# Half a row of x in the last step as two transfers of 88 and 40 partitions, and the first result stored in three pieces

## The chip, the cores and the metric

The kernel runs on one core of a Trainium2 chip. The metric is the device time of one execution in microseconds. All data is float32. The engines that matter are VectorE (DVE in the profile), ScalarE (ACT), SyncE (SP), which issues most transfers, and the core's sixteen DMA engines, which carry every transfer between HBM and SBUF.

## The reference

x and y have the shape 8 × 4096 × 512. Only the diagonal of x·yᵀ is needed: 8 × 4096 dot products of 512 elements, then a softmax over the 4096 of each batch.

```
gram = np.matmul(x, y.transpose(0, 2, 1))
diag = np.diagonal(gram, axis1=1, axis2=2)
diag = diag - diag.max(axis=-1, keepdims=True)
exp = np.exp(diag)
return (exp / exp.sum(axis=-1, keepdims=True)).astype(np.float32)
```

## The kernel before

The eight batches are worked in two sets of four. A set fills the 128 partitions: each batch has 32 partitions (G), and each partition holds 128 consecutive rows (C) of its batch. A set is read in four steps of 32 rows (R), so there are eight steps (S), t = 0 to 7. A step loads 32 rows of x into one of two buffers (`xs`) and 32 rows of y into the only y buffer (`ys`), 8.4 MB each: 64 KB for each partition.

Steps 0 to 5 load x and y whole. VectorE multiplies (`products`, L75) and sums the rows (`sums`, L78), and ScalarE sums the last two rows (`sums_act`, L83). ScalarE copies the last six rows of y aside (L125), so that `ys` comes free sooner. Step 6 loads y in two parts.

Step 7, the last, is loaded in ever smaller parts, x and y in turn, all issued on SyncE's queue: x rows 0–14, y rows 0–16, x 15–22, y 17–24, x 23–27, y 25–28, x 28–29, y 29–30. Then come x row 30 with the first 192 elements of row 31 (L162, 352 KB), y row 31, and the last 320 elements of x row 31 (L164, 160 KB). Each row is one instruction on VectorE, which multiplies and sums (`dot`, L87), as soon as both its rows are there. Row 31 is two instructions, of 192 and of 320 elements; the second takes up the first one's result through an extra element, where y has a 1. Ahead of row 29 the largest of the earlier dot products is taken (`largest`, L100).

The first set's softmax is done early, in steps 3 and 4. Its result, `res[0]`, is stored by SyncE after all loads are issued, in five pieces of 32, 32, 32, 16 and 16 partitions (L173). After the last dot product come the second set's softmax (`exps`, `normalize`) and its store from ScalarE's queue (L175).

The semaphores that tell of a transfer's completion are eight, used in turn by SyncE's and ScalarE's transfers alike. A transfer is not issued before the one that had its semaphore, the eighth before it, has landed. Queued transfers start in the order of their issue.

Of the kernel before, what the change touches and what calls it, by code (L numbers as in the profile page):

```python
# [1 line left out]

# [5 lines left out]


@with_exitstack
def kernel(
    ctx: ExitStack,
    tc: tile.TileContext,
    x: bass.AP,
    y: bass.AP,
    out: bass.AP,
):
    nc = tc.nc
    ctx.enter_context(tc.manual_schedule())  # L20
    f32 = mybir.dt.float32
    Alu = mybir.AluOpType
    Act = mybir.ActivationFunctionType
    X = mybir.AxisListType.X
    B, N, D = x.shape
    P = nc.NUM_PARTITIONS
    G = 32
    Q = P // G
    C = N // G
    R = 32  # L30
    K = 6
    W = 2
    F = 17
    V = 8
    L = 320
    S = B // Q * (C // R)


    xv = x.rearrange("(s b) (j c) d -> s (b j) c d", b=Q, j=G)
    yv = y.rearrange("(s b) (j c) d -> s (b j) c d", b=Q, j=G)  # L40
    ov = out.rearrange("(s b) (j c) -> s (b j) c", b=Q, j=G)

    big = ctx.enter_context(tc.tile_pool(name="big", bufs=1))
    small = ctx.enter_context(tc.tile_pool(name="small", bufs=1))


    xs = [big.tile([P, R * D + i], f32, name=f"xs{i}") for i in range(2)]
    ys = big.tile([P, R * D + 1], f32, name="ys")
    side = big.tile([P, K * D], f32, name="side")

    diag = [small.tile([P, C + i], f32, name=f"diag{i}") for i in range(B // Q)]
    res = [small.tile([P, C], f32, name=f"res{i}") for i in range(B // Q)]

    def columns(t, r0, n):
        c0 = t % (C // R) * R + r0
        return slice(c0, c0 + n)

    def rows(tile_, r0, n):
        return tile_[:, r0 * D : (r0 + n) * D].rearrange("p (r d) -> p r d", d=D)

    def dots_of(t, r0, n):
        return diag[t * R // C][:, columns(t, r0, n)]

    def load(tile_, view, t, r0, n):
        nc.sync.dma_start(out=rows(tile_, r0, n), in_=view[t * R // C, :, columns(t, r0, n), :])  # L65

    def load_x(t, r0, n):
        load(xs[t % 2], xv, t, r0, n)

    def load_y(t, r0, n):  # L70
        load(ys, yv, t, r0, n)

    def products(t, r0, n, yt):
        xt = rows(xs[t % 2], r0, n)
        nc.vector.tensor_tensor(out=xt, in0=xt, in1=yt, op=Alu.mult)  # L75

    def sums(t, r0, n):
        nc.vector.tensor_reduce(out=dots_of(t, r0, n), in_=rows(xs[t % 2], r0, n), axis=X, op=Alu.add)  # L78

    def sums_act(t, r0, n):  # L80
        for r in range(r0, r0 + n):
            row = xs[t % 2][:, r * D : (r + 1) * D]
            nc.scalar.activation(out=row, in_=row, func=Act.Copy, accum_out=dots_of(t, r, 1))  # L83

    def dot(t, e0, n, got):
        xt = xs[t % 2][:, e0 : e0 + n]
        nc.vector.scalar_tensor_tensor(  # L87
            out=xt, in0=xt, scalar=1.0, in1=ys[:, e0 : e0 + n], op0=Alu.mult, op1=Alu.mult, accum_out=got
        )

    def over_quadrant(name, column, op, negate=False):

        got = small.tile([P, 1], f32, name=name)
        nc.vector.tensor_reduce(  # L94
            out=got, in_=column.to_broadcast([P, G]), axis=X, op=op, negate=negate, apply_transpose=True
        )
        return got

    def largest(out, d):
        nc.vector.tensor_reduce(out=out, in_=d, axis=X, op=Alu.max)  # L100

    def exps(i, d):
        mxp = small.tile([P, 1], f32, name=f"mxp{i}")
        largest(mxp, d)
        nmx = over_quadrant(f"nmx{i}", mxp, Alu.max, negate=True)
        sump = small.tile([P, 1], f32, name=f"sump{i}")
        nc.scalar.activation(out=res[i], in_=diag[i][:, :C], func=Act.Exp, bias=nmx, scale=1.0, accum_out=sump)  # L107
        return sump

    def normalize(i, sump):  # L110
        total = over_quadrant(f"sum{i}", sump, Alu.add)
        rc = small.tile([P, 1], f32, name=f"rc{i}")
        nc.vector.reciprocal(out=rc, in_=total)  # L113
        nc.vector.tensor_single_scalar(out=res[i], in_=res[i], scalar=rc, op=Alu.mult)  # L114

    nc.vector.addr_align(128, offset=0, max_nops=0)
    nc.scalar.addr_align(128, offset=0, max_nops=0)
    nc.sync.drain()  # L120

    for t in range(S - 2):
        load_x(t, 0, R)
        load_y(t, 0, R)
        nc.scalar.activation(out=side, in_=ys[:, (R - K) * D : R * D], func=Act.Copy)  # L125
        if t == C // R:
            normalize(0, sump)
        products(t, 0, R - K, rows(ys, 0, R - K))
        products(t, R - K, K, rows(side, 0, K))
        sums(t, 0, R - W)  # L130
        sums_act(t, R - W, W)
        if t == C // R - 1:
            sump = exps(0, diag[0])

    t = S - 2
    load_x(t, 0, R)
    for r0, n in ((0, F), (F, R - F)):
        load_y(t, r0, n)
        products(t, r0, n, rows(ys, r0, n))
    sums(t, R - V, V)  # L140
    sums_act(t, 0, R - V)

    t += 1
    nc.vector.memset(ys[:, R * D : R * D + 1], 1.0)
    x1, y1, done = 0, 0, 0
    for n, m in ((15, F), (8, 8), (5, 4), (2, 2)):
        for tile_, view, r0, k in ((xs[t % 2], xv, x1, n), (ys, yv, y1, m)):
            load(tile_, view, t, r0, k)
            if tile_ is ys:
                y1 += m  # L150
            else:
                x1 += n
            while done < min(x1, y1):
                if done == R - 3:
                    largest(diag[1][:, C:], diag[1][:, : C - 4])
                dot(t, done * D, D, dots_of(t, done, 1))
                done += 1
    E = R * D
    cut = E - L
    tail = xv[t * R // C].rearrange("p c d -> p (c d)")  # L160
    o = columns(t, 0, R).start * D
    nc.sync.dma_start(out=xs[t % 2][:, x1 * D : cut], in_=tail[:, o + x1 * D : o + cut])  # L162
    load_y(t, y1, R - y1)
    nc.sync.dma_start(out=xs[t % 2][:, cut:E], in_=tail[:, o + cut : o + E])  # L164
    dot(t, (R - 2) * D, D, dots_of(t, R - 2, 1))
    dot(t, (R - 1) * D, D - L, xs[t % 2][:, E:])
    dot(t, cut, L + 1, dots_of(t, R - 1, 1))

    met = small.tile([P, C - R], f32, name="met")
    nc.scalar.activation(out=met, in_=diag[1][:, : C - R], func=Act.Copy)  # L170

    for p, n in ((0, G), (G, G), (2 * G, G), (3 * G, 16), (3 * G + 16, 16)):
        nc.sync.dma_start(out=ov[0, p : p + n, :], in_=res[0][p : p + n, :])  # L173
    normalize(1, exps(1, diag[1][:, C - 4 :]))
    nc.scalar.dma_start(out=ov[1], in_=res[1])  # L175


# [1 line left out]
_INS = ['x', 'y']  # L179
_OUTS = [((8, 4096), 'float32')]  # L180


# [23 lines left out]
```

## Time and profile before

| | us |
|---|---|
| median of 3 runs | 320.6 |
| lowest and highest run | 320.45, 321.18 |
| the profiled execution, its own time | 320.27 |
| its span, first to last instruction | 318.5 |
| VectorE busy | 244.7 |
| ScalarE busy | 42.0 |

The profiled execution's time is 1.8 us more than its span. The span's HBM traffic is 134.22 MB read and 0.13 MB written.

The profile's issues of the last step, with the median time from issue to landing, show how long transfers stand in the queue:

```profile
xs<-in_x_dram SPq DMA_DIRECT2D x1, 2048.0 KB, 20.0
...
xs<-in_x_dram SPq DMA_DIRECT2D x1, 352.0 KB, 23.9
ys<-in_y_dram SPq DMA_DIRECT2D x1, 256.0 KB, 19.5
xs<-in_x_dram SPq DMA_DIRECT2D x1, 160.0 KB, 15.0
out_dram<-res ACTq DMA_DIRECT2D x1, 64.0 KB, 1.6
```

Columns: what is written and read, the issuing queue, the number of issues, KB of each, and us to landing. The first line is the transfer that the change divides. The 160 KB of the last piece spend 15 us on the way, nearly all of it behind other transfers; the last store, with nothing ahead of it, takes 1.6 us.

### The profile page before, as it was taken

The page shows a single profiled execution, that of the slowest core. Times are in us where ns is not written, and L with a number is a line of the kernel's source. Part 1 is how long each engine was busy: PE and PEld are TensorE (multiplying, and loading weights), DVE is VectorE, ACT ScalarE, POOL GpSimd, SP SyncE. Part 2 cuts the span into 40 slices and gives each one's busy share as a digit, 9 for nine tenths or more (in the row PEclk, how much of TensorE's full clock was granted, in tenths as well). Part 3 has the DMA queues.
Part 4 walks back from the last instruction along what each step waited for, and adds up shares of the span by engine and source line. Part 5 has one row for each costly group of instructions (what it writes and reads, how often), then busy time and mean ns, then how long its engine had stood idle before and what let it go on. Part 6 is the DMA issues. An engine that isn't in the chain of part 4 may idle for free.

```text
span 318.5 us, 304 instructions
## 1 busy us (share of the span) xinstructions
DVE 244.7 (77%) x99; ACT 42.0 (13%) x84; POOL 0.2 (0%) x4
## 2 busy tenths in 40 slices
DVE  0000069995899939999399994999939999996995
ACT  1000030100301003010120103000030100098000
POOL 0000000000000000000000000000000000000000
DMA  9999999999999999999999999999999899999993
GB/s 389 403 395 486 436 395 453 469 395 395 502 420 395 477 444 395 428 494 395 395 486 436 395 444 477 395 403 486 428 395 477 383 429 432 432 443 407 425 412 128
DMA packets 4098, 134.37 MB, mean 422 GB/s; under 512 B 512, under 2 KB 896, under 8 KB 1408
## 3 DMA queue, kind: packets, MB, share of 16 engines
q1 hardware_dynamic: 3952, 134.29, 97.9%
q10 hardware_dynamic: 144, 0.07, 0.1%
q14 instruction: 2, 0.02, 0.0%
HBM read 134.22 MB, written 0.13 MB: 422 GB/s over the span
## 4 chain that ended last, share of the span: by engine, by line
DMA 62%; DVE 35%; issue 2%; SPq 0%; ACT 0%; DVEq 0%
DMA ys<-in_y_dram 51%; DVE xs L75 30%; DMA xs<-in_x_dram 11%; DVE diag L78 4%; SPq L65 0%; DVE xs L87 0%; DVE res L114 0%; DVE sum L94 0%; DVE nmx L94 0%; ACT res L107 0%; DVE rc L113 0%; DVE mxp L100 0%; DVEq L75 0%; DVEq L87 0%; SPq L120 0%
## 5 line engine op out<-in xcount | busy, mean ns | idle before, releaser
L75 DVE TENSOR_TENSOR xs<-xs,ys 128x13312 f32<-128x13312 f32 (+2 forms) x8 | 101.4, 12690 | 66.3 <-DMA ys<-in_y_dram 66.3
L78 DVE TENSOR_REDUCE diag<-xs 128x30 f32<-128x15360 f32 (+1 forms) x7 | 101.3, 14477 | 0.2
L83 ACT ACTIVATE xs<-xs 128x512 f32<-128x512 f32 x36 | 22.2, 616 | 111.5 <-DVE xs L75 111.5
L125 ACT ACTIVATE side<-ys 128x3072 f32<-128x3072 f32 x6 | 16.6, 2766 | 123.7 <-DMA ys<-in_y_dram 123.7
L87 DVE SCALAR_TENSOR_TENSOR xs<-xs,ys 128x512 f32<-128x512 f32 (+2 forms) x33 | 20.1, 673 | 3.2 <-DMA ys<-in_y_dram 3.0
L75 DVE TENSOR_TENSOR xs<-xs,side 128x3072 f32<-128x3072 f32 x6 | 20.1, 3351 | 0.0
L83 ACT ACTIVATION_READ_ACCUMULATOR xs<-xs 128x1 f32 x36 | 6.7, 185 | 0.0
L107 ACT ACTIVATE res<-diag,nmx 128x128 f32<-128x128 f32 x2 | 0.8, 402 | 36.9 <-DVE nmx L94 36.9
L87 DVE DVE_READ_ACCUMULATOR xs<-xs,ys 128x1 f32 x33 | 2.8, 83 | 0.0
L125 ACT ACT_TABLE_LOAD x1 | 1.3, 1283 | 1.2 <-PEq L190 1.2
L94 DVE TRANSPOSE_TENSOR_REDUCE sum<-sump 128x1 f32<-128x32 f32 x2 | 0.4, 211 | 1.2 <-ACT res L107 1.2
L114 DVE TENSOR_SCALAR res<-res,rc 128x128 f32<-128x128 f32 x2 | 0.6, 286 | 0.1
L100 DVE TENSOR_REDUCE mxp<-diag 128x1 f32<-128x128 f32 (+1 forms) x2 | 0.4, 222 | 0.1
L94 DVE TRANSPOSE_TENSOR_REDUCE nmx<-mxp 128x1 f32<-128x32 f32 x2 | 0.4, 212 | 0.1
L113 DVE RECIPROCAL rc<-sum 128x1 f32<-128x1 f32 x2 | 0.3, 164 | 0.1
L107 ACT ACTIVATION_READ_ACCUMULATOR res<-diag,nmx 128x1 f32 x2 | 0.4, 186 | 0.0
L170 ACT ACTIVATE met<-diag 128x96 f32<-128x96 f32 x1 | 0.3, 282 | 0.0
L100 DVE TENSOR_REDUCE diag<-diag 128x1 f32<-128x124 f32 x1 | 0.3, 275 | 0.0
L190 POOL MEMSET const-bfloat16-1.0<- 128x1 bf16 x1 | 0.1, 102 | 0.0
L190 POOL MEMSET const-uint8-127<- 128x1 uint8 x1 | 0.1, 102 | 0.0
L190 POOL MEMSET const-float32-0.0<- 128x1 f32 x1 | 0.1, 100 | 0.2 <-issue 0.2
L190 POOL MEMSET const-float32-1.0<- 128x1 f32 x1 | 0.1, 99 | 0.0
(1 smaller groups left out, 0.1 us busy)
## 6 DMA issues: line engine op xcount, KB each, us to landing
ys<-in_y_dram SPq DMA_DIRECT2D x2, 4352.0 KB, 15.5
ys<-in_y_dram SPq DMA_DIRECT2D x1, 3840.0 KB, 24.3
xs<-in_x_dram SPq DMA_DIRECT2D x1, 3840.0 KB, 14.3
xs<-in_x_dram SPq DMA_DIRECT2D x1, 2048.0 KB, 20.0
ys<-in_y_dram SPq DMA_DIRECT2D x1, 2048.0 KB, 17.2
xs<-in_x_dram SPq DMA_DIRECT2D x1, 1280.0 KB, 19.9
ys<-in_y_dram SPq DMA_DIRECT2D x1, 1024.0 KB, 21.9
xs<-in_x_dram SPq DMA_DIRECT2D x1, 512.0 KB, 22.7
```

The costliest lines, as they stand in the source:

```text
L75: nc.vector.tensor_tensor(out=xt, in0=xt, in1=yt, op=Alu.mult)
L78: nc.vector.tensor_reduce(out=dots_of(t, r0, n), in_=rows(xs[t % 2], r0, n), axis=X, op=Alu.add)
L83: nc.scalar.activation(out=row, in_=row, func=Act.Copy, accum_out=dots_of(t, r, 1))
L87: nc.vector.scalar_tensor_tensor(out=xt, in0=xt, scalar=1.0, in1=ys[:, e0 : e0 + n], op0=Alu.mult, op1=Alu.mult, accum_out=got)
L94: nc.vector.tensor_reduce(out=got, in_=column.to_broadcast([P, G]), axis=X, op=op, negate=negate, apply_transpose=True)
L100: nc.vector.tensor_reduce(out=out, in_=d, axis=X, op=Alu.max)
L107: nc.scalar.activation(out=res[i], in_=diag[i][:, :C], func=Act.Exp, bias=nmx, scale=1.0, accum_out=sump)
L113: nc.vector.reciprocal(out=rc, in_=total)
L114: nc.vector.tensor_single_scalar(out=res[i], in_=res[i], scalar=rc, op=Alu.mult)
L125: nc.scalar.activation(out=side, in_=ys[:, (R - K) * D : R * D], func=Act.Copy)
L170: nc.scalar.activation(out=met, in_=diag[1][:, : C - R], func=Act.Copy)
L190: nc = _bacc.Bacc("TRN2", target_bir_lowering=False, num_devices=1)
```

## The change

The load of x rows 15–22 (2048 KB, 16 KB for each partition) becomes three transfers: the first seven and a half rows in all 128 partitions, then the last 256 elements (H) of row 22 in partitions 0–87 (M), then the same elements in partitions 88–127. These small transfers have 1 KB for each partition. The order of the loads is otherwise kept. The first set's result is stored in three pieces of 32, 32 and 64 partitions. The number of SyncE's transfers is the same as before, two more loads and two fewer stores. `tail`, `o` and the two transfers of L162 and L164 are written with a new helper, without a change to what they move.

```
+    H = 256
+    M = 88
...
+    tail = xv[t * R // C].rearrange("p c d -> p (c d)")
+    o = columns(t, 0, R).start * D
+
+    def load_tail(e0, e1, p0=0, p1=P):
+        nc.sync.dma_start(out=xs[t % 2][p0:p1, e0:e1], in_=tail[p0:p1, o + e0 : o + e1])
...
-            load(tile_, view, t, r0, k)
+            if tile_ is not ys and n == 8:
+                e1 = (r0 + k) * D
+                load_tail(r0 * D, e1 - H)
+                load_tail(e1 - H, e1, 0, M)
+                load_tail(e1 - H, e1, M, P)
+            else:
+                load(tile_, view, t, r0, k)
...
-    nc.sync.dma_start(out=xs[t % 2][:, x1 * D : cut], in_=tail[:, o + x1 * D : o + cut])
+    load_tail(x1 * D, cut)
     load_y(t, y1, R - y1)
-    nc.sync.dma_start(out=xs[t % 2][:, cut:E], in_=tail[:, o + cut : o + E])
+    load_tail(cut, E)
...
-    for p, n in ((0, G), (G, G), (2 * G, G), (3 * G, 16), (3 * G + 16, 16)):
+    for p, n in ((0, G), (G, G), (2 * G, 2 * G)):
         nc.sync.dma_start(out=ov[0, p : p + n, :], in_=res[0][p : p + n, :])
```

## The prediction

> **What bounds the kernel now.** I read the page first. One core streams 134 MB from HBM, and the mean rate over the span hardly differs from the rate of a full slice; the slices of DMA are all nines but the last.
>
> ```profile
> span 318.5 us, 304 instructions
> DVE 244.7 (77%) x99; ACT 42.0 (13%) x84; POOL 0.2 (0%) x4
> DMA  9999999999999999999999999999999899999993
> DMA packets 4098, 134.37 MB, mean 422 GB/s; under 512 B 512, under 2 KB 896, under 8 KB 1408
> ```
>
> The bytes are the same after the change, so only what follows the last bytes can move. The chain of waits from 293 us on says which transfer ends it: the 320-element piece of x (L164, 160 KB). VectorE's last product starts 0.09 us after it lands.
>
> ```profile
> 298.76 14.99 DMA xs<-in_x_dram
> 313.75 0.03 issue
> 313.78 0.02 DVEq L87
> 313.80 0.04 issue
> 313.84 0.51 DVE xs L87 x2
> ```
>
> The timeline of VectorE shows how much room stands before that. Products of 512 follow at 0.61 us each without a gap until row 25.
>
> ```profile
> 308.57 0.69 DVE L87 SCALAR_TENSOR_TENSOR xs<-xs,ys 128x512 f32<-128x512 f32 x1
> ...
> 309.24 0.69 DVE L87 SCALAR_TENSOR_TENSOR xs<-xs,ys 128x512 f32<-128x512 f32 x1
> ...
> 311.89 0.68 DVE L87 SCALAR_TENSOR_TENSOR xs<-xs,ys 128x512 f32<-128x512 f32 x1
> ...
> 312.70 0.69 DVE L87 SCALAR_TENSOR_TENSOR xs<-xs,ys 128x512 f32<-128x512 f32 x1
> ...
> 313.36 0.36 DVE L87 SCALAR_TENSOR_TENSOR xs<-xs,ys 128x192 f32<-128x192 f32 x1
> ```
>
> Row 25 starts 0.06 us later than the pace (309.24 for 309.18), row 30 0.20 us late (312.70 for 311.89 + 0.61 = 312.50), and the two pieces of row 31 follow as their data lands. From 312.5 us the DMA sets the pace; VectorE alone could be done 0.39 us sooner: 309.18 for 309.24 is 0.06, so row 30 at 312.44, the 192 piece at 313.05, its sum read out 0.36 later as now (313.64 + 0.08 for 313.36), the last, which takes that sum up, 0.04 behind it at 313.45 for 313.84.
>
> Last, the DMA view of 312 to 314 us, in slices of 0.05 us: the sixteen engines do not stop together.
>
> ```profile
> DMA  8999999999999997697754332232100000000000
> ```
>
> From 313.05 to 313.35 us only two to three tenths are busy: four or five engines of sixteen still work. The trace's records of completion say the same. Each transfer's semaphore counts to sixteen, one count for each engine; these are the sixteen counts of L164's transfer, sorted (us):
>
> ```
> 312.97 313.02 313.11 313.14 313.16 313.25 313.25 313.26 313.28 313.29 313.34
> 313.53 313.68 313.69 313.70 313.75
> ```
>
> Eleven early ones, a gap of 0.19, five late ones. Every load of the kernel has this pattern (first to last 0.74 to 0.84 us), and it dates from the first transfer: its sixteen first packets begin between 1.80 and 2.52 us, and the five that begin last (2.21, 2.27, 2.33, 2.40, 2.52) are also last at their second packets (5.30 to 5.57, the others by 5.14). After that all keep one pace. Each transfer waits for its late five.
>
> **The change, part by part.** *Half a row on eleven engines.* The transfer of x rows 15 to 22 had 8 packets of 16 KB for each of sixteen engines. It becomes 8 of 15 KB on each, plus 128 of 1 KB: 88 on eleven engines (the change's own words), 8 each, and 40, which eleven can't share evenly; I take ten with 4 each (eight with 5 each would add one packet, 0.05 us). Packet times in the trace: 512 B 27 ns, 1280 B 55, 2048 B 86, 10 KB 389, 16 KB 615. On the straight lines between neighbours 1 KB is 27 + 28 × 512/768 = 46 ns and 15 KB 389 + 226 × 5/6 = 577.
> - Five engines that carry none: 8 × (577 − 615) = −0.30 us.
> - Ten with twelve: −0.30 + 12 × 0.046 = +0.25. The lower bound, if a packet's fixed part were hidden, is 4 × 615/16 ns = +0.15; the upper, with two further completion writes of 9 ns, +0.27. I take 0.25: the fixed part shows in the spacing of landings (312.68 − 311.79 = 0.89 for 8 × 113 ns).
> - One with eight: −0.30 + 0.37 = +0.07.
>
> Everything behind on each engine moves by that much. If the five that carry none are the late five, L164's counts become at most 313.29 + 0.25 = 313.54 for the ten, 313.34 + 0.07 = 313.41 for the eleventh, 313.75 − 0.30 = 313.45 for the five: it lands at 313.54, **0.21 us sooner** (0.30 with the lower bound, where the five are last; 0.19 with the upper). The same sum for the 352 KB piece (early ten by 312.22, last 312.68): 312.47; for the last row of y (312.90, 313.33): 313.15. VectorE follows: row 30 at 312.49 (0.02 after landing, as now), the 192 piece at 313.18 (0.03 after), the last at 313.54 + 0.09 = 313.63 for 313.84. What comes after it is unchanged to the end of the span.
>
> That the idle engines are the late ones is not in the trace, which has no engine numbers. I infer it: one issue starts sixteen engines over 0.72 us, so they are started in some order; if that is by number, and the eleven are the first, the five left out are those started last.
>
> *SyncE's queue.* A transfer waits for the eighth before it, whose semaphore it uses again:
>
> ```profile
> 288.76 0.38 SPq L162 DMA_DIRECT2D xs<-in_x_dram  x1
> 293.86 0.33 SPq L65 DMA_DIRECT2D ys<-in_y_dram  x1
> 298.76 0.33 SPq L164 DMA_DIRECT2D xs<-in_x_dram  x1
> 303.65 8.47 SPq L173 DMA_DIRECT2D out_dram<-res  x5
> ```
>
> Two more issues of 0.43 us fall at about 279 us and push all later ones two places on. The two-row load of y, issued at 288.23 now, waits for the landing at 293.84; the 352 KB piece, y's last row and L164 wait for the 15 KB part and the two small ones, near 298.5, and go out by 299.5, the last 0.7 us later than now. At that time the loads that land at 303.63, 306.72, 309.22, 310.50 and 311.79 are still queued, 12 us of work, so nothing runs dry: no cost. Without that cover L164's 0.7 us would be on the path.
>
> *Three stores for five.* Same bytes. The first is issued as before, with the landing at 303.63, the others at two later landings, all behind L164's packets. They land by 314.64 now; the final store is issued at 316.11. Cost and gain nothing, hidden under 1.5 us of softmax. Row 22's product has two more semaphores to wait for; they are set by 299 us, it runs near 307.3.
>
> **Sum:** 320.27 of the profiled execution − 0.21 = 320.06. The median of the runs shown is 0.33 above that execution, so 320.6 − 0.21 = **320.4**.
>
> **Rivals.**
> *The pieces are spread over all sixteen* (the change doesn't do what it says). Then each engine has 8 × 577 + 8 × 46 for 8 × 615 ns, +0.07, and two more completion writes, 0.02: 320.7. For: every transfer seen ends on sixteen counts. Against: the change's words. The Trainium skill ("DMA: Bandwidth & Descriptors", "Rules for kernel authors") says this of two transfers to disjoint partition halves: both use all sixteen engines, so don't bother. The same page ("Why a DMA increments its semaphore by 16 and not by 1") says that the count is the largest up to 16 that divides the partitions, on the lowest-numbered engines, 11 and 10 here; that agrees with my forecast. No run here shows either.
>
> *The small packets go at half pace* (slower). Eleven engines write 88 partitions in another assignment than in the 128-partition loads, so two may write into one place of SBUF at once. At half pace the twelve cost 0.55 more: the ten move by 0.80, to 314.09, 0.34 later than now: 320.9. It decides from 313.75 − 313.29 = 0.46 us on early engines. For: all loads seen use one pattern. Against: nothing seen; the 32-partition stores have another shape but end in an idle stretch. The Trainium skill ("SBUF — State Buffer", "Door 1: The DMA port swizzle") has partitions 32 apart share a port, which with blocks of eight partitions would put engines in pairs on a port; no trace here shows it.
>
> *The late five are not those left out.* A late carrier moves by 0.25: lands at 314.00, 320.6 + 0.25 = 320.85. For: the starts' order isn't tied to numbers. Against: exactly five begin late and stay late.
>
> *One engine takes a piece alone:* 128 × 46 ns − 0.30 = 5.6 us more on it, 326. For: nothing but that such a shape isn't in the trace.
>
> **How the numbers follow.** Forecast 0.53 (its own range 320.1 to 320.7: gain 0.19 to 0.30, and the runs' scatter, which reaches 0.15 under the median), spread over sixteen 0.12, half pace 0.14, late carriers 0.14, one engine 0.03, something else 0.04. Range: down to 320.05, the largest gain of 0.30 with 0.25 of scatter; up to 321.0, half pace with little more. 0.2% is 0.64 us, about what a measurement of this kernel can tell from no change. The forecast and three rivals lie within it. Faster by more: 0.08, by scatter alone, since VectorE's room and the 0.30 both end below 0.64. Slower by more: 0.03 for one engine and 0.07 for a worse conflict or scatter. Same: 0.82.
>
> **What would show it.** Step by step: the sixteen counts of L164's transfer within 0.6 us for 0.78, the last near 313.54; the last product at 313.63; in the DMA view no stretch of two to three tenths before the end; packets of 1 KB at 46 ns (90 for half pace); SyncE's issue of the two-row y at 293.86, and L164's by 299.5 with no idle DMA after. I am wrong if L164 lands after 313.75, if the counts keep five late ones, or if VectorE starts row 30 before 312.44.

## The result and the profile after

| | before | after |
|---|---|---|
| median | 320.6 us (14 runs) | 321.33 us (14 runs) |
| lowest and highest run | 320.21, 321.18 | 320.96, 322.17 |
| profiled execution, its own time | 320.27 us | 321.36 us |
| its span | 318.5 us | 319.6 us |

The changed kernel is slower: the ratio is 1.0024, with a 95% interval of 1.0016 to 1.0032, or 0.5 to 1.0 us. The prediction was 320.4, with a range up to 321.0.

The page of the changed kernel: the same bytes in more and smaller packets, VectorE's and ScalarE's busy time as before (244.9 and 42.0 us), and a lower mean rate.

```profile
span 319.6 us, 305 instructions
DVE 244.9 (77%) x99; ACT 42.0 (13%) x84; POOL 0.2 (0%) x4
DMA packets 4215, 134.37 MB, mean 420 GB/s; under 512 B 501, under 2 KB 1013, under 8 KB 1525
```

The chain of waits from 294 us on. Columns: start, duration (us), what.

```profile
299.31 14.49 DMA xs<-in_x_dram
313.80 0.02 issue
313.83 1.03 DVE xs L89 x4
314.86 0.04 issue
314.90 0.51 DVE xs L89 x2
```

The 352 KB piece, not the last one, now sits in the chain: it lands at 313.80 where it landed at 312.68, and VectorE is behind it without a break until the last product starts, at 314.90 for 313.84. L164's transfer (in the helper of L151 now) lands at 314.81 for 313.75. The timeline of VectorE shows the loss earlier:

```profile
309.03 0.69 DVE L89 SCALAR_TENSOR_TENSOR xs<-xs,ys 128x512 f32<-128x512 f32 x1
...
310.34 0.69 DVE L89 SCALAR_TENSOR_TENSOR xs<-xs,ys 128x512 f32<-128x512 f32 x1 [0.61 <-DMA ys<-in_y_dram]
...
313.83 0.69 DVE L89 SCALAR_TENSOR_TENSOR xs<-xs,ys 128x512 f32<-128x512 f32 x1
```

VectorE stands idle for 0.61 us ahead of row 25 (0.06 before), since every load behind the divided one is late. So the loss lies in the DMA near the divided load. Two views of half-microseconds around it, first of the kernel before, then of the changed one (columns: stretch, its length, busy time of VectorE, ScalarE and GpSimd with instructions, clock, DMA share, GB/s):

```profile
297.50:298.00 0.50, 0.50 (x3) 0.00 (x0) 0.00 (x0) 1.00 1.01 426
298.00:298.50 0.50, 0.50 (x3) 0.00 (x0) 0.00 (x0) 1.00 1.23 524
298.50:299.00 0.50, 0.50 (x3) 0.00 (x0) 0.00 (x0) 1.00 1.00 426
299.00:299.50 0.50, 0.50 (x3) 0.00 (x0) 0.00 (x0) 1.00 0.85 360
```

```profile
297.50:298.00 0.50, 0.50 (x3) 0.00 (x0) 0.00 (x0) 1.00 0.94 305
298.00:298.50 0.50, 0.50 (x1) 0.00 (x0) 0.00 (x0) 1.00 1.92 486
298.50:299.00 0.50, 0.50 (x3) 0.00 (x0) 0.00 (x0) 1.00 0.40 113
299.00:299.50 0.50, 0.50 (x3) 0.00 (x0) 0.00 (x0) 1.00 1.24 465
```

A packet counts where it starts, so single rows swing, but two things can be read. From 298.0 to 298.5 the packets take 1.92 times the stretch on sixteen engines and bring 486 GB/s; before, 1.23 brought 524: they take longer for each byte. And the mean of these four rows is 342 GB/s where it was 434. The DMA engines are busy and move less. The trace's packets near 298 us (293 to 303 us) say which (longest, ns; usual is the median of the same size elsewhere, for 1 KB that of e3 below):

```
            usual   longest before   longest after   sum over the usual, after
1 KB           46                -              94   1.4 us
15 KB         573                -             761   0.7 us
16 KB         615              622            1071   7.1 us
```

About half of the small packets keep their 46 ns, and the slowest take twice that; the 16 KB packets of the y load behind them lose far more. Together that is 9.2 us of engine time, 0.57 us for each of sixteen engines.

Counts of completion settle who carried what. The piece of 88 partitions has one increment at its issue (280.11) and then eleven single counts; the piece of 40 has one (280.50) and ten:

```
88: 298.66 298.66 298.76 298.92 298.98 299.02 299.04 299.10 299.17 299.30 299.74
40: 298.94 298.97 299.06 299.21 299.27 299.29 299.34 299.38 299.42 299.93
L164: 313.77 313.89 314.00 314.12 314.13 314.15 314.20 314.27 314.30 314.32 314.33 314.37 314.40 314.42 314.43 314.81
```

The shares are as the prediction took them. The Trainium skill ("DMA: Bandwidth & Descriptors", "Why a DMA increments its semaphore by 16 and not by 1") gives 11 and 10 by its rule, with the rest of the semaphore's sixteen added at the issue; the trace agrees in the counts and in the time of that increment (its size isn't in the trace). But one engine is last in both pieces, 0.44 and 0.51 us behind the next. It is a carrier, an engine that takes a share of both, and L164 waits for one engine alone.

Two parts of the 1.06 us by which L164 lands later can be told apart in the profiled executions. The 17-row y load, which stands in the queue ahead of all that the change divides, lands at 294.20 for 293.84: 0.36 is there ahead of the divided load. From that landing to L164's it takes 20.61 us for 19.91: **0.70 us** is from the divided load. The latter is close to the 0.73 of the medians, and is the measure for the experiments below. It goes by the last engine of each load, which need not be the same one.

### The profile page after: what moved, and what is told of

Read it like the earlier page. It is cut to its first block, busy times and chain, and to the rows that moved or that the text cites. A ratio compares the mean times of both kernels' runs of the same rounds, so it can differ in the third digit from the quotient of the medians.

```text
span 319.6 us, 305 instructions
## 1 busy us (share of the span) xinstructions
DVE 244.9 (77%) x99; ACT 42.0 (13%) x84; POOL 0.2 (0%) x4
## 4 chain that ended last, share of the span: by engine, by line
DMA 62%; DVE 35%; issue 2%; SPq 0%; ACT 0%; DVEq 0%
DMA ys<-in_y_dram 51%; DVE xs L77 30%; DMA xs<-in_x_dram 11%; DVE diag L80 4%; DVE xs L89 0%; SPq L67 0%; DVE res L116 0%; DVE sum L96 0%; DVE nmx L96 0%; ACT res L109 0%; DVE rc L115 0%; DVE mxp L102 0%; DVEq L77 0%; SPq L151 0%; SPq L122 0%
```

## The experiments

Theories. **1:** the pieces are written by engines in another assignment than the loads beside them, and that holds up all engines. **2:** late engines are among those that carry more. **3:** the stores. The table has, for each run, the median against that of the kernel before on the same chip, the ratio with its 95% interval, and from the profile the time between the last count of the 17-row y load and that of L164's ("y to L164").

| run | median, before | ratio | y to L164 |
|---|---|---|---|
| before | 320.6 | | 19.91 |
| changed kernel | 321.33, 320.6 | 1.0024 (1.0016–1.0032) | 20.61 |
| e1_split_alone | 321.36, 320.62 | 1.0022 (1.0013–1.0031) | 20.61 |
| e2_stores_alone | 320.68, 320.62 | 1.0000 (0.9991–1.0009) | 19.87 |
| e3_one_piece | 320.70, 320.62 | 1.0001 (0.9992–1.0010) | 19.94 |
| e4_80_and_48 | 321.08, 320.62 | 1.0012 (1.0003–1.0021) | 20.39 |
| e5_small_load_0_63 | 321.89, 320.36 | 1.0045 (1.0033–1.0058) | 21.19 |
| e6_small_load_32_95 | 320.88, 320.36 | 1.0013 (1.0004–1.0022) | 20.21 |
| e7_whole_row_88_40 | 321.66, 320.36 | 1.0038 (1.0025–1.0051) | 21.20 |
| e8_stores_88_40 | 320.59, 320.36 | 1.0007 (0.9997–1.0017) | 19.92 |
| e9_ten_engines_32_71 | 320.91, 320.63 | 1.0012 (1.0001–1.0023) | 20.17 |
| e10_ten_engines_88_127 | 321.58, 320.63 | 1.0030 (1.0019–1.0042) | 20.75 |

**The two halves of the change.** e1 is the changed kernel with the five stores back:

```
-    for p, n in ((0, G), (G, G), (2 * G, 2 * G)):
+    for p, n in ((0, G), (G, G), (2 * G, G), (3 * G, 16), (3 * G + 16, 16)):
```

> The divided load alone; the first result is stored in five pieces again. Theory 1 (the two 1 KB pieces are written by engines in another assignment than the loads beside them, and hold up all engines): all of the loss stays, 0.6 to 0.8 us over the kernel before, and the packets near 298 us are slow as in the changed kernel (1 KB up to 0.09 us, 16 KB up to 1.07 us). Theory 2 (late engines are among those that carry more): also 0.6 to 0.8 us, but with packets of the usual length. Theory 3 (the stores): within 0.2 us of the kernel before.

It took 321.36: all of the loss, with 1 KB packets up to 0.106 us and 16 KB packets up to 1.00. e2 is the kernel before with the three stores:

> The load of 16 KB for each partition is whole again; the three stores stay. Theories 1 and 2: within 0.2 us of the kernel before, every 16 KB packet at 0.61 to 0.62 us. Theory 3: 0.5 us or more over it. The counts of the y load that lands near 294 us tell besides whether eleven early and five late engines come back in another execution with undivided loads; the prediction takes them to be fixed.

It took 320.68, and its longest 16 KB packet 622 ns. Theory 3 falls; the stores cost nothing that the runs can tell (0.06 us, with an interval of 0.3 to either side). The eleven-and-five pattern did not come back: the y load's counts rise evenly from 293.06 to 293.85, with no gap over 0.17 us.

**Small packets, in the usual assignment.** e3 brings the same 1 KB pieces in one transfer of 128 partitions:

```
                 load_tail(r0 * D, e1 - H)
-                load_tail(e1 - H, e1, 0, M)
-                load_tail(e1 - H, e1, M, P)
+                load_tail(e1 - H, e1)
...
-    for p, n in ((0, G), (G, G), (2 * G, 2 * G)):
+    for p, n in ((0, G), (G, G), (2 * G, G), (3 * G, G)):
```

> The last 256 elements of row 22 come in one transfer of all 128 partitions, the first result in four stores, so that SyncE's transfers are as many as before. The 1 KB packets are the same 128, but each engine has eight, to the partitions that it writes in every other load. Theory 1: no hold-up, 0.05 to 0.15 us over the kernel before, which is eight more packets for each engine (8 x 577 + 8 x 46 for 8 x 615 ns is 0.07) and a completion write. Theory 2: the same, for no engine carries more. If small packets as such hold up the engines: 0.4 us or more.

No hold-up: 320.70, 0.03 us more from landing to landing, no 1 KB packet over 48 ns, no 16 KB packet over 652. That the packets are small is not the cause, and the prediction's price of 46 ns holds in this assignment.

**Even bytes, another assignment.** e4 cuts at 80 instead of 88:

```
-    M = 88
+    M = 80
```

> The two pieces are of 80 and 48 partitions, which sixteen engines can share evenly, 5 and 3 each, so that each engine has the same bytes as before, but in blocks of partitions other than those of a 128-partition load. Theory 1: a hold-up, slow 1 KB and 16 KB packets near 298 us, 0.3 to 0.8 us over the kernel before. Theory 2: no engine carries more, 0.05 to 0.2 us over it, packets of the usual length. The two theories are told apart here.

Both pieces now end on sixteen counts, so every engine carries the bytes of before. Still 0.46 us are lost on the median and 0.48 from landing to landing, with 1 KB packets up to 76 ns and 16 KB packets up to 947. Theory 2 can't do that, and theory 1 has most of the loss. The remaining 0.22 us to the changed kernel's 0.70 is not the carrier's alone, for which the prediction's sum has 0.25: the packets near 298 us exceed the usual times by 7.6 us of engine time in e4 and by 9.2 in the changed kernel, 0.47 and 0.57 for each of sixteen engines. About 0.10 of the 0.22 can so be more hold-up.

**Which place, or which count?** e5 and e6 leave the 16 KB load whole and add one small transfer behind it, into a buffer that is free by then, with four stores; they differ in its partitions alone. e5's additional lines are:

```
+            if tile_ is not ys and n == 8:
+                nc.sync.dma_start(out=side[0:64, 0:D], in_=tail[0:64, o + r0 * D : o + (r0 + 1) * D])
```

> The 16 KB load is whole; behind it an additional transfer brings row 15 of x (2 KB for each partition) for partitions 0 to 63 into a buffer that nothing reads any more. Four stores, so SyncE's transfers are as many as before. Its own packets cost each of sixteen engines 4 x 0.086 = 0.34 us, whatever the theory. Theory 1a (what clashes are the places in SBUF: the Trainium skill's page SBUF — State Buffer, Door 1: The DMA port swizzle, has partitions 0 to 63 on eight of sixteen ports): packets near 298 us are slow, and it takes 0.6 us or more over the kernel before. Theory 1b (any transfer with a share other than eight partitions for each engine holds up the others): as slow as its twin with partitions 32 to 95, whatever that is.

> The same additional transfer, for partitions 32 to 95. Bytes, packets and their share for each engine (four) are those of the twin with partitions 0 to 63. Theory 1a: by the port map these partitions reach all sixteen ports, four on each, and no packet is slow: 0.3 to 0.4 us over the kernel before, and less than the twin by 0.2 us or more. Theory 1b: as slow as the twin, to within 0.15 us.

For equal bytes, packets and engines, 0 to 63 costs 1.53 us and 32 to 95 costs 0.52 on the medians; from landing to landing 1.28 and 0.30 (e6's own packets were to cost 0.34; its median's interval is 0.13 to 0.70). The half-microseconds of both, with the columns of above, e5 first:

```profile
297.50:298.00 0.50, 0.50 (x3) 0.00 (x0) 0.00 (x0) 1.00 1.15 336
298.00:298.50 0.50, 0.50 (x3) 0.00 (x0) 0.00 (x0) 1.00 1.36 299
298.50:299.00 0.50, 0.50 (x3) 0.00 (x0) 0.00 (x0) 1.00 0.83 197
299.00:299.50 0.50, 0.50 (x3) 0.00 (x0) 0.00 (x0) 1.00 1.06 303
```

```profile
297.50:298.00 0.50, 0.50 (x3) 0.00 (x0) 0.00 (x0) 1.00 1.00 402
298.00:298.50 0.50, 0.50 (x3) 0.00 (x0) 0.00 (x0) 1.00 1.11 455
298.50:299.00 0.50, 0.50 (x3) 0.00 (x0) 0.00 (x0) 1.00 0.92 385
299.00:299.50 0.50, 0.50 (x3) 0.00 (x0) 0.00 (x0) 1.00 1.08 459
```

In e5 a DMA share of 1.36 brings 299 GB/s, in e6 1.11 brings 455. The longest packets near 298 us are 187 ns (2 KB) and 1265 ns (16 KB) in e5, 86 and 627 in e6, close to the usual ones. The map of SBUF's ports in the Trainium skill ("SBUF — State Buffer", "Door 1: The DMA port swizzle") puts partitions 0 to 63 on eight of sixteen ports and 32 to 95 on all sixteen; the runs agree.

e9 and e10 are the same addition with 40 partitions, as in the change's second piece, 32 to 71 and 88 to 127; this is e10's edit of e5's line:

```
-                nc.sync.dma_start(out=side[0:64, 0:D], in_=tail[0:64, o + r0 * D : o + (r0 + 1) * D])
+                nc.sync.dma_start(out=side[88:128, 0:D], in_=tail[88:128, o + r0 * D : o + (r0 + 1) * D])
```

> The additional transfer of 2 KB for each partition now has 40 partitions, 32 to 71, as many as the second piece of the change, and so ten engines with four each. By the map of SBUF's ports in the Trainium skill (SBUF — State Buffer, Door 1: The DMA port swizzle) they reach ten ports, four partitions on each. If the place alone decides: no slow packets, every 2 KB packet under 0.10 us and every 16 KB packet under 0.66, and from the y load's last landing near 294 us to L164's last 19.9 to 20.3 us (ten engines have 0.34 more). If a count under sixteen is what holds up the engines: packets near 298 us as slow as with partitions 0 to 63, and 20.5 us or more.

> The same with partitions 88 to 127, those of the change's second piece. By the same map they lie on eight of sixteen ports. If the place decides: slow 2 KB and 16 KB packets near 298 us, and 0.2 us or more longer from landing to landing than with 32 to 71. If the count decides: as with 32 to 71.

Both have ten counts. 32 to 71: 20.17 us from landing to landing, near 298 us no 2 KB packet over 86 ns, no 16 KB packet over 627. 88 to 127: 20.75 us, packets up to 191 and 1080 ns, and 0.67 us more on the median. The place decides, not the count of engines. A count under sixteen by itself held up nothing.

The slow packets come close to accounting for the landing. The time by which the packets near 298 us exceed the usual, shared among sixteen engines, comes to 0.06 us in e3, 0.47 in e4, 0.89 in e5, 0.54 in e10 and under 0.01 in e6 and e9. With the 0.34 of the additional transfer's own packets (4 × 0.086), that gives 1.23 us in e5, 0.88 in e10 and 0.34 in e6 and e9. Measured from landing to landing: 0.03 in e3, 0.48 in e4, 1.28 in e5, 0.84 in e10, 0.30 in e6 and 0.26 in e9.

Two things were not separated. Which engine writes which partitions isn't in the traces, so that two engines meet in one place is inferred. And a transfer to other partitions also reads other rows in HBM; that the place in SBUF matters, and not the one in HBM, rests on the port map having told the outcome of four runs beforehand.

**The size.** e7 is the changed kernel with the whole of row 22 divided:

```
-    H = 256
+    H = 512
```

> As the changed kernel, but the divided piece is the whole row 22, 2 KB for each partition. Theory 1 with a hold-up in proportion to the bytes: the part that is the same for all engines (about 0.48 us, from the run with 80 and 48 partitions) doubles, and a carrier's extra bytes cost 12 x 0.086 - 8 x (615 - 535)/1000 = 0.39 us: 1.2 to 1.5 us over the kernel before. With a hold-up for each clash whatever its size: 0.48 + 0.39, so 0.8 to 1.0 us. Theory 2 alone: 0.39 us.

1.30 us on the medians and 1.29 from landing to landing, within the 1.2 to 1.5 of a hold-up in proportion to the bytes. The packets near 298 us exceed the usual by 16.7 us here, 1.05 for each engine; with the 0.39 that was forecast for a carrier that would be 1.44, more than was lost.

**Which engines are late.** e8 is the kernel before, with two stores:

```
-    for p, n in ((0, G), (G, G), (2 * G, G), (3 * G, 16), (3 * G + 16, 16)):
+    for p, n in ((0, 88), (88, 40)):
```

> The kernel before, with the first result stored in two pieces of 88 and 40 partitions behind all loads. It tells which engines are late: the store of 88 partitions has eleven counts, each about 0.2 us behind the same engine's count of L164's transfer. If the prediction's inference holds, these follow the eleven early counts, and the five late engines show none. If late engines are among the first eleven, late counts show in the stores too. The time is that of the kernel before, within 0.3 us, for the stores end under the softmax.

The median is 0.23 us over the kernel before, with an interval that takes in no change at all. The counts of L164's transfer and of the store of 88 partitions (without its increment at the issue):

```
L164:  313.63 313.70 313.72 313.75 313.76 313.77 313.78 313.85 313.89 313.90 313.94 314.08 314.10 314.15 314.29 314.36
store: 313.83 313.88 313.92 313.93 313.94 313.97 313.98 314.04 314.07 314.09 314.54
```

Each store count follows one of L164's by about 0.2 us. Ten follow the ten earliest; the eleventh follows the very last. The engines left out are those at 313.94 and 314.08 to 314.29. So four of the five late engines are left out, but the latest is a carrier. The same holds in e9: its ten counts end at 298.60 and then 299.34. In the kernel before itself this was not recorded.

## Why the prediction was wrong, step by step

The prediction named a landing of L164 after 313.75 as a sign that it is wrong; the transfer landed at 314.81.

- **The bound, and where the time is decided:** right. The bytes and VectorE's time stayed; L164's landing moved by 1.06 us and the last product's start by 1.06.
- **Shares and packet prices:** right where nothing clashes. Eleven and ten counts; 15 KB packets took 573 ns for 577, 1 KB packets 46 for 46 in e3.
- **"Everything behind on each engine moves by that much":** this step failed first. It let each engine run at its own pace, and priced the small packets by rows in which every engine writes the partitions of a 128-partition load. In the other assignment they took up to 94 ns and held up the packets beside them. e4, with even bytes, shows 0.48 us of it, where a sum of packet times has 0.1 at most; e6 and e9 show that it goes away when the place is changed.
- **The rival of half pace:** its cause, two engines in one place of SBUF, fits the runs, and its price does not. It charged ten carriers 0.55 us each for their small packets and left the rest of the queue at its pace. In the changed kernel the 1 KB packets lost 1.4 us of engine time in all, and the 16 KB packets 7.1. It was given a chance of 0.14, for want of a row in which a load is written otherwise; the Trainium skill's port map, which stood beside it, agrees with e5, e6, e9 and e10.
- **"If the five that carry none are the late five":** failed too. The pattern of eleven and five was read off one execution. In e8 four of the five late engines are left out, but the last one sets the landing, and it carries, as the last engine of the changed kernel does. That was the rival "the late five are not those left out" for one engine. Its price, 0.25, isn't shown by itself: with the 0.57 of hold-up it gives 0.82 us, for 0.70 measured.
- **The two rivals were priced as alternatives.** Each alone gave 320.85 to 320.9, within the range; they came together, and the time is beyond it. That 320.6 + 0.25 + 0.55 = 321.4 is near the measured 321.33 is luck, for the hold-up lay mostly in other packets than those it charged.
- **SyncE's queue:** right. The two-row y load went out at 294.22 with the landing at 294.20, L164's at 300.16 (299.5 forecast), and the loads behind were still queued. The stores ended at 315.37, ahead of the final store at 317.17.

What stays open: the 0.36 us by which the 17-row y load lands later in the profiled execution of the changed kernel. It is there in the profiles of all runs but e2 and e7 (294.11 to 294.44 against 293.85 and 293.91); in e1, e3 and e4 one engine is alone behind from the first transfer on. e3's median is only 0.08 us over the kernel before, with an interval of ±0.3, so these runs don't tell whether the timed executions have that delay. Open too is how much of the changed kernel's 0.70 us is a carrier's share.

## What to carry to other kernels

Where the DMA is busy throughout, a transfer to part of the partitions can cost more than its own packets, by slowing the full-size packets beside it. Here partitions 0 to 63 and 88 to 127 did so, while 32 to 95 and 32 to 71 cost their own packets and no more. Look at the packets next to the change, not only at those changed. Before moving bytes from late engines to early ones, find out in the changed kernel's own counts which engines are late; a pattern from one execution of another program isn't enough.

## What the runs showed of the hardware that was not expected

A few small packets can take more from others than they last: in e5 64 packets of 2 KB, which usually take 86 ns, 5.5 us in all, came with 12.6 us of additional time in 16 KB packets, one of which took 1265 ns for 615. Moving the same transfer by 32 partitions left 0.1 us of it. And a transfer on ten or eleven engines has only their single counts when its data lands; the one other increment of its semaphore comes at its issue (280.11 and 280.50 in the changed kernel, some 18 us ahead of the data).
